# Claiming every SBUF slot in a fixed order before a two-layer hybrid decoder trunk starts

## The chip, the cores and the metric

The kernel runs on one core of a Trainium2 chip. The metric is the device time of one execution in microseconds (us). Engines are named as in the profile: PE is TensorE (matmuls), PEld its weight loads, DVE is VectorE, ACT is ScalarE, POOL is GpSimd, SP is SyncE, which here only issues DMAs.

## The reference

Two layers work on one sequence of 256 tokens, 1,024 channels wide, in float32. Each layer is a token mixer and a feed-forward block, both behind an RMSNorm:

```python
h = rmsnorm(x, norm_mix[l]); proj = h @ w_in[l]          # 1024 -> 5956 columns, split in 12 parts
y_attn = dsa_attention(aq, ak, av, iq, ik, iw)           # 8 heads of 64; an indexer picks 64 keys per query
o = hgrn2_chunked(silu(hq), k_in, hi, log_f)             # gated linear recurrence, 4 heads, state 128 x 128
y_hgrn = rmsnorm(o, hgrn_norm[l]) * silu(hg)
merged = sigmoid(ga) * (y_attn @ w_proj_attn[l]) + sigmoid(gb) * (y_hgrn @ w_proj_hgrn[l])
x = x + merged @ w_out[l]                                # 1024 -> 1024
h = rmsnorm(x, norm_ffn[l])
g, u = split(h @ w_ffn_in[l])                            # 1024 -> 2 x 2816
x = x + (silu(g) * u) @ w_ffn_out[l]                     # 2816 -> 1024
```

## The kernel before, in words

**Tiling.** The 256 tokens are two blocks `i` of 128. All products with the model's weights go through one pattern. `take()` brings a chunk of a weight matrix into SBUF by DMA (`w`, 128 partitions x 2,048 float32, 8 KB per partition), ACT rounds it to `hi` (float32r), and DVE writes the rest `lo = w - hi`. The activations are held transposed and split in the same way: `hT`, `h2T`, `yT`, `mT` and `act`, each a hi and a lo part. `mm3` then issues three matmuls per slice, hi x hi, hi x lo and lo x hi, to get nearly float32 precision out of the fast float32r mode.

**Who reads what.** In these matmuls the *activations are the stationary operand* (PEld loads a 128 x 128 slice of them, 512 bytes per partition, before every matmul, 188 ns by the profile) and the *weights `hi` and `lo` are the moving operand* (512 columns, 2,048 bytes per partition). A row of the trace such as `fi<-hi,h2T_lo` therefore reads: output `fi`, moving `hi`, stationary `h2T_lo`. For each layer there are 1,512 such matmuls of 512 columns, 3,024 in all, and 48 of 324 columns (`idx`, 96 in all).

**Stages of a layer, by the names of their outputs.** `idx`, `aq`, `ak`, `hf`, `hq`, `av`, `vh`, `hg`, `ga`, `gb` (parts of the input projection, with the attention and the recurrence in between); `pj` (the two output projections of the mixer, stationary `yT`); `wo` (stationary `mT`); `fi` (feed-forward in, 528 matmuls, stationary `h2T`); `fo` (feed-forward out, 264 matmuls, 24 for each of eleven tiles `act`).

**Order.** The program is first recorded. `Program.schedule` then simulates it, picks the order of the instructions, and gives every tile a *slot* of its tag: three slots each for `w`, `hi` and `lo`, eight (4 KB) for the stationary pairs (tag `hT`), fourteen (4 KB) for large tiles (tag `s4`, which holds `act` among others), six for 2 KB tiles (`s2`), fourteen for small vectors (`sm`). `emit` then walks through that order and asks the tile pool for each tile as it comes up, with the tag and the slot as its key. The pool places a key in SBUF when it first sees it, behind what it has placed before. So the addresses before follow from the order in which the schedule first touches each slot: constants of 8, 32 or 64 bytes stand between the large tiles.

Line 442 in the trace is the line of `emit` that issues every recorded call, so nearly all rows carry it; the tiles' names tell the rows apart.

Of the kernel before, what the change touches and what calls it, by code (L numbers as in the profile page):

```python
# [8 lines left out]
BF16 = mybir.dt.bfloat16  # L9
F32 = mybir.dt.float32  # L10
F32R = mybir.dt.float32r
I32 = mybir.dt.int32
U8 = mybir.dt.uint8
# [140 lines left out]
class Program:  # L154
# [54 lines left out]
    def price(self, op, eng, name, out, args, kw):  # L209
# [23 lines left out]
        n = max([n] + [v.size for v in ins])  # L233
        if name in ("tensor_copy", "tensor_scalar") and not any(v.t.tag in PSUM_TAGS for v in ins if isinstance(v, View)):
            return 65.0 + n * 0.52
# [190 lines left out]
        return self.span  # L426


    def emit(self, tc):
        nc = tc.nc  # L430
        engines = {"DVE": nc.vector, "ACT": nc.scalar, "PE": nc.tensor, "SP": nc.sync, "POOL": nc.gpsimd}
        with ExitStack() as ctx:
            sb = ctx.enter_context(tc.tile_pool(name="sb", bufs=1))
            ps = ctx.enter_context(tc.tile_pool(name="ps", bufs=1, space=PSUM))
            ctx.enter_context(tc.manual_schedule())
            real = lambda v: v.resolve() if isinstance(v, View) else v
            for o in self.order:
                for t in o.first:
                    pool = ps if t.tag in PSUM_TAGS else sb
                    t.handle = pool.tile([128] + list(t.shape), t.dtype, tag=f"{t.tag}_{t.slot}", name=t.name)  # L440
                for name, a, k in o.calls:
                    getattr(engines[o.eng], name)(*[real(x) for x in a], **{n: real(x) for n, x in k.items()})  # L442


PSUM_TAGS = ("P", "Q")
SLOTS = {"w": 3, "hi": 3, "lo": 3, "hT": 8, "s4": 14, "s2": 6, "sm": 14, "work": 2, "bias": 2, "rqs": 4,
         "gbc": 2, "P": 4, "Q": 4}
TUNING = {"stretch": 1.5, "bonus": 3000.0, "slack": 4000.0}
# [727 lines left out]
```

## Time and profile before

| | before |
|---|---|
| median of 3 runs | 821.86 us (820.89 to 822.17) |
| the profiled execution's own time | 822.42 us |
| its span, first to last instruction | 820.5 us |
| outside the span | 1.9 us |
| PE busy | 807.7 us (98%), 3,982 matmul records |
| PEld busy | 659.8 us (80%) |
| DVE busy | 537.8 us (66%) |
| ACT busy | 403.2 us (49%) |
| DMA | 139.66 MB, 51% of 16 engines' time |

Matmuls are pipelined: a matmul of 512 columns has a record of 387 to 401 ns, yet the next one starts 227 to 235 ns later. The pace of PE is therefore read from the *starts* of successive matmuls, not from their durations. In the timeline a row "x3" is three matmuls of the same kind that follow each other, and in the chain view a row "x36" is 36 matmuls back to back, with the time from the first start to the next work's start.

### The profile page before, as it was taken

How to read it: one execution, taken by the hardware profiler on the slowest of the kernel's cores; microseconds unless marked ns; L12 is line 12 of the kernel's file. 1: busy time of each engine (PE TensorE's matmuls, PEld its weight loads, DVE VectorE, ACT ScalarE, POOL GpSimd, SP SyncE). 2: the span in 40 equal slices, each digit the busy share in tenths (PEclk: the TensorE clock that was granted, in tenths of full speed). 3: DMA queues.
4: the chain of work that ended last, by engine and by line, in shares of the span. 5: the costliest groups of instructions: out<-in, count | busy, mean ns of one | idle time of the engine just before them, and what ended most of it. 6: DMA issues, size and time to landing. Idle time of an engine off the chain costs nothing.

```text
span 820.5 us, 10255 instructions
## 1 busy us (share of the span) xinstructions
PE 807.7 (98%) x3982; PEld 659.8 (80%) x3982; DVE 537.8 (66%) x947; ACT 403.2 (49%) x518; POOL 5.3 (1%) x13
## 2 busy tenths in 40 slices
PE   7999999999999999999999999999999999999998
PEld 5887788888878888888887778888887888888886
DVE  5999855677775454554488998566868645556442
ACT  5765855343364445452346676533435544445330
POOL 2000000000000000000000000000000000000000
PEclk7999999999999999999999999999999999999999
DMA  8645455333656556546546365543354665655531
GB/s 277 207 148 203 146 174 196 103 112 123 218 190 204 175 185 194 167 153 206 166 154 231 103 206 189 170 146 112 103 195 155 214 198 166 201 179 180 175 133 51
DMA packets 86224, 139.66 MB, mean 170 GB/s; under 512 B 3214, under 2 KB 50480, under 8 KB 86176
## 3 DMA queue, kind: packets, MB, share of 16 engines
q1 hardware_dynamic: 85856, 138.53, 50.9%
q0 software_dynamic: 320, 0.48, 0.3%
q8 instruction: 31, 0.51, 0.3%
q14 instruction: 17, 0.14, 0.0%
HBM read 137.95 MB, written 1.05 MB: 169 GB/s over the span
## 4 chain that ended last, share of the span: by engine, by line
PE 89%; DVE 6%; issue 2%; ACT 2%; DMA 1%; POOL 0%; DVEq 0%; POOLq 0%
PE fi L442 29%; PE fo L442 15%; PE pj L442 5%; PE gb L442 5%; PE wo L442 5%; PE ga L442 4%; PE av L442 3%; PE aq L442 3%; PE hg L442 3%; PE vh L442 3%; PE hq L442 2%; DVE lo L442 2%; PE ak L442 2%; PE idx L442 2%; PE hf L442 1%
## 5 line engine op out<-in xcount | busy, mean ns | idle before, releaser
L442 DVE TENSOR_TENSOR lo<-w,hi 128x2048 fp32r<-128x2048 f32 (+3 forms) x134 | 295.0, 2202 | 222.0 <-ACT hi L442 221.6
L442 ACT ACTIVATE hi<-w 128x2048 fp32r<-128x2048 f32 (+3 forms) x134 | 247.4, 1846 | 284.7 <-PE fi L442 96.4
L442 PE MATMUL fi<-hi,h2T_hi 128*128 128x512 f32 x352 | 141.1, 401 | 0.2
L442 PE MATMUL fi<-hi,h2T_lo 128*128 128x512 f32 x352 | 138.2, 393 | 0.0
L442 PE MATMUL fi<-lo,h2T_hi 128*128 128x512 f32 x352 | 137.7, 391 | 0.0
L442 PE MATMUL fo<-hi,act 128*128 128x512 f32 x352 | 111.4, 395 | 0.0
L442 PEld LDWEIGHTS fi<-hi,h2T_lo 128*128 128x128 f32 x352 | 66.1, 188 | 15.3 <-DVE h2T_lo L442 0.7
L442 PEld LDWEIGHTS fo<-hi,act 128*128 128x128 f32 x352 | 66.1, 188 | 14.9
L442 PEld LDWEIGHTS fi<-hi,h2T_hi 128*128 128x128 f32 x352 | 66.1, 188 | 13.8 <-DVE h2T_lo L442 0.8
L442 PEld LDWEIGHTS fi<-lo,h2T_hi 128*128 128x128 f32 x352 | 66.2, 188 | 13.2
L442 PE MATMUL fo<-lo,act 128*128 128x512 f32 x176 | 69.1, 392 | 0.0
L442 PEld LDWEIGHTS fo<-lo,act 128*128 128x128 f32 x176 | 33.1, 188 | 7.4
L442 PE MATMUL gb<-hi,hT_hi 128*128 128x512 f32 x64 | 26.8, 418 | 0.0
L442 PE MATMUL pj<-hi,yT_hi 128*128 128x512 f32 x64 | 26.0, 407 | 0.0
L442 PE MATMUL wo<-hi,mT_hi 128*128 128x512 f32 x64 | 25.8, 404 | 0.0
L442 PE MATMUL ga<-hi,hT_hi 128*128 128x512 f32 x64 | 25.7, 402 | 0.0
L442 PE MATMUL pj<-hi,yT_lo 128*128 128x512 f32 x64 | 25.3, 395 | 0.0
L442 PE MATMUL pj<-lo,yT_hi 128*128 128x512 f32 x64 | 25.2, 394 | 0.0
L442 PE MATMUL gb<-hi,hT_lo 128*128 128x512 f32 x64 | 25.2, 393 | 0.0
L442 PE MATMUL ga<-hi,hT_lo 128*128 128x512 f32 x64 | 25.1, 393 | 0.0
L442 PE MATMUL wo<-lo,mT_hi 128*128 128x512 f32 x64 | 25.1, 392 | 0.0
L442 PE MATMUL ga<-lo,hT_hi 128*128 128x512 f32 x64 | 25.1, 392 | 0.0
(346 smaller groups left out, 1309.9 us busy)
## 6 DMA issues: line engine op xcount, KB each, us to landing
w<-in_w_ffn_in_dram SPq DMA_DIRECT2D x88, 512.0 KB, 4.7
w<-in_w_in_dram SPq DMA_DIRECT2D x42, 1024.0 KB, 5.1
w<-in_w_ffn_out_dram SPq DMA_DIRECT2D x22, 1024.0 KB, 4.7
w<-in_w_out_dram SPq DMA_DIRECT2D x8, 1024.0 KB, 4.7
w<-in_w_proj_attn_dram SPq DMA_DIRECT2D x4, 1024.0 KB, 4.9
w<-in_w_proj_hgrn_dram SPq DMA_DIRECT2D x4, 1024.0 KB, 4.9
w<-in_w_in_dram SPq DMA_DIRECT2D x4, 512.0 KB, 11.4
w<-in_w_in_dram SPq DMA_DIRECT2D x4, 324.0 KB, 10.8
```

What stands on the lines that cost most here:

```text
L442: getattr(engines[o.eng], name)(*[real(x) for x in a], **{n: real(x) for n, x in k.items()})
```

## The change

A new method `homes` runs at the head of `emit`. It asks the pool once for every SBUF slot, in an order of its own, before any instruction is issued: first small slots up to address 24,576 (with a pad up to exactly that address), then the slots of `w`, `hi`, `lo`, `hT`, `s4` and `gbc`, then everything else from large to small. The tiles that `emit` asks for later find their key already placed. The schedule, the slots, the instructions of every engine, their order and their waits are the same as before, instruction by instruction; only addresses differ.

```diff
+    def homes(self, pool):
+        size = {}
+        for tag, q in self.queue.items():
+            for t in q:
+                if tag not in PSUM_TAGS:
+                    key = (tag, t.slot)
+                    size[key] = max(size.get(key, 0), t.n * SIZE.get(t.dtype, 4))
+        big = [k for tag in ("w", "hi", "lo", "hT", "s4", "gbc") for k in sorted(size) if k[0] == tag]
+        rest = sorted((k for k in size if k not in big), key=lambda k: (size[k], k))
+        at, low = BASE, []
+        for k in rest:
+            n = -(-size[k] // 32) * 32
+            if at + n <= ORIGIN:
+                low.append((k, size[k]))
+                at += n
+        low.reverse()
+        named = {k for k, _ in low}
+        if at < ORIGIN:
+            low.append((("pad", 0), ORIGIN - at))
+        for (tag, slot), n in low + [(k, size[k]) for k in big + [k for k in reversed(rest) if k not in named]]:
+            pool.tile([128, -(-n // 4)], F32, tag=f"{tag}_{slot}", name=f"home_{tag}{slot}")
...
             real = lambda v: v.resolve() if isinstance(v, View) else v
+            self.homes(sb)
             for o in self.order:
...
+SIZE = {U8: 1, BF16: 2}
+BASE, ORIGIN = 16512, 24576
```

The addresses of what PE reads in the 3,024 large matmuls, taken from the two built programs. A byte address counts within a partition; "remainder" is the address modulo 128. Slices of a stationary tile lie 512 bytes apart and columns of a moving tile 2,048 bytes, so the remainder of a slot is that of all its slices.

| operand | slots before (hex) | remainder before | slots after (hex) | remainder after |
|---|---|---|---|---|
| moving `hi` | 1abc0, 1e4c0, 244c0 | 64 | c000, e000, 10000 | 0 |
| moving `lo` | 204c0, 224c0, 264c0 | 64 | 12000, 14000, 16000 | 0 |
| stationary, tag `hT`, four slots | 107c0, 137c0, 19bc0, 1cbc0 | 64 | 18000 to 1f000 in steps of 1000 | 0 |
| stationary, tag `hT`, the other four | 2bbe0, 2cbe0, 31be0, 32be0 | 96 | (the same range) | 0 |
| stationary `act`, tag `s4` | d3c0, e3c0, f7c0, 147c0 | 64 | 20000 to 2b000 in steps of 1000 | 0 |
| stationary `act`, tag `s4` | a380, b380 | 0 | (the same range) | 0 |
| stationary `act`, tag `s4` | 8360, 9360, 2dbe0, 2ebe0, 2fbe0, 30be0 | 96 | (the same range) | 0 |

By the slots that the schedule gave, the stationary operand of the 3,024 matmuls has these remainders before: 64 in 1,944 of them, 0 in 72, and 96 in 1,008. The 1,008 are: in layer 0, the whole of `pj` (96), half of `wo` (48) and of `fi` (264), and 132 of `fo`; in layer 1, half of the ten input projections but `idx` (264: 24 each of `aq`, `ak`, `hf`, `hq`, `av`, `vh`, `hg` and 48 each of `ga` and `gb`), half of `pj` (48), and 156 of `fo`. In `fi` and `wo` of layer 1 there are none.

## Rows read from the trace of the kernel before

**Rows 1.** The page: engines' busy time, share of the span, instructions; the granted clock.

```profile
PE 807.7 (98%) x3982; PEld 659.8 (80%) x3982; DVE 537.8 (66%) x947; ACT 403.2 (49%) x518; POOL 5.3 (1%) x13
...
PEclk7999999999999999999999999999999999999999
```

**Rows 2.** The page: the chain that ended last, by engine.

```profile
PE 89%; DVE 6%; issue 2%; ACT 2%; DMA 1%; POOL 0%; DVEq 0%; POOLq 0%
```

**Rows 3.** Waits: who waited for whom, us in total, times, longest.

```profile
DVE lo L442 <- ACT hi L442: 221.6, 91, 5.7
ACT hi L442 <- PE fi L442: 96.4, 42, 3.9
```

**Rows 4.** The chain, layer 0, `fi`: start us, us, what.

```profile
232.57 3.06 PE fi L442 x12
...
236.06 39.42 PE fi L442 x171
...
278.70 8.29 PE fi L442 x36
...
356.31 1.45 PE fo L442 x6
```

**Rows 5.** The chain, layer 1, the same pieces of `fi`.

```profile
633.22 3.02 PE fi L442 x12
...
636.67 38.82 PE fi L442 x171
...
678.70 8.19 PE fi L442 x36
...
755.59 1.46 PE fo L442 x6
```

**Rows 6.** The chain, layer 0: a stretch of `ga` and one of `pj`.

```profile
116.71 8.16 PE ga L442 x36
...
194.22 9.81 PE pj L442 x42
```

**Rows 7.** PE's timeline in `fo`: start us, us; stationary remainder 96, tile `act3`.

```profile
374.05 0.86 PE L442 MATMUL fo<-hi,act 128*128 128x512 f32 x3
...
376.85 0.86 PE L442 MATMUL fo<-hi,act 128*128 128x512 f32 x3
```

**Rows 8.** The same, remainder 0, tile `act4`.

```profile
379.64 0.85 PE L442 MATMUL fo<-hi,act 128*128 128x512 f32 x3
...
382.39 0.85 PE L442 MATMUL fo<-hi,act 128*128 128x512 f32 x3
```

**Rows 9.** The same, remainder 64, tile `act6`.

```profile
392.11 0.84 PE L442 MATMUL fo<-hi,act 128*128 128x512 f32 x3
...
394.83 0.84 PE L442 MATMUL fo<-hi,act 128*128 128x512 f32 x3
```

**Rows 10.** PE's timeline behind transposes, `fi` of layer 1, remainder 64.

```profile
636.74 0.40 PE L442 MATMUL fi<-lo,h2T_hi 128*128 128x512 f32 x1
...
638.60 0.39 PE L442 MATMUL fi<-hi,h2T_hi 128*128 128x512 f32 x1
...
640.87 0.39 PE L442 MATMUL fi<-lo,h2T_hi 128*128 128x512 f32 x1
```

**Rows 11.** Windows at both clock levels: us, PE busy (x instructions), PEclk, DMA share, GB/s.

```profile
64.10:67.30 3.20, 3.20 (x9) 0.50 0.73 229
...
636.00:676.00 40.00, 40.00 (x181) 1.00 0.63 202
```

**Rows 12.** PE's timeline at the lower clock: `hq`, 512 columns.

```profile
64.22 0.63 PE L442 MATMUL hq<-lo,hT_hi 128*128 128x512 f32 x1
...
66.78 0.63 PE L442 MATMUL hq<-lo,hT_hi 128*128 128x512 f32 x1
```

**Rows 13.** PE's timeline: `idx`, 324 columns, layer 1, full clock, remainder 96.

```profile
419.06 0.31 PE L442 MATMUL idx<-hi,hT_lo 128*128 128x324 f32 x1
...
422.03 0.31 PE L442 MATMUL idx<-lo,hT_hi 128*128 128x324 f32 x1
```

**Rows 14.** All loads and conversions of one kind: ns min/median/max, first and last start us.

```profile
L442 PEld LDWEIGHTS fo<-lo,act x176: 187/188/192, 356.2 to 815.9; 128*128 128x128 f32 x176
...
L442 DVE TENSOR_TENSOR lo<-w,hi x134: 822/2293/2295, 13.9 to 802.0; 128x2048 fp32r<-128x2048 f32 x124, 128x648 fp32r<-128x648 f32 x4, 128x1024 fp32r<-128x1024 f32 x4, 128x1296 fp32r<-128x1296 f32 x2
```

**Rows 15.** Windows of `fi`, layer 0: us, busy PE, PEld, DVE, ACT, POOL, PEclk, DMA share.

```profile
232.50:356.00 123.50, 123.43 (x558) 100.49 (x559) 68.61 (x78) 56.67 (x64) 0.00 (x0) 1.00 0.59 189
```

## The prediction

> **What bounds the kernel now.** I read the page first. PE is busy for 98% of the span and the clock is full in all but the first slices [rows 1]; the chain that ended last runs over PE for 89% [rows 2]. Then the waits: DVE waits for ACT, and ACT for PE to give a buffer back [rows 3]. In `fi` of layer 0 PE has 123.43 of 123.50 us, DVE 68.61 and ACT 56.67, DMA a share of 0.59 [rows 15]. So PE sets the pace, and almost any nanosecond that a matmul saves shortens the run. What is left is the pace itself, read from the distance of starts.
>
> **That pace depends on where the stationary operand lies.** Three tiles of `fo` are used one after the other by the same code. The two rows of each group enclose 12 matmuls:
> - remainder 96: 376.85 - 374.05 = 2.80 us, 233.3 ns each [rows 7];
> - remainder 0: 382.39 - 379.64 = 2.75 us, 229.2 ns [rows 8];
> - remainder 64: 394.83 - 392.11 = 2.72 us, 226.7 ns [rows 9].
>
> Other stages agree: `pj` of layer 0 (remainder 96 throughout) takes 9.81 / 42 = 233.6 ns, `ga` of layer 0 (64 throughout) 8.16 / 36 = 226.7 ns [rows 6]. `fi` is the cleanest pair, because both layers run the same pieces: 171 matmuls take 39.42 us in layer 0, where 84 of them have remainder 96, and 38.82 us in layer 1, where none has [rows 4, 5].
>
> All moving operands have remainder 64 before. So remainder 64 is not the roundest address, it is the one that *agrees with the moving operand*; the rounder 0 is slower by 2.5 ns. I read this as: two streams out of SBUF get in each other's way least when both sit at the same place within a block of 128 bytes. The weight load itself lasts 187 to 192 ns wherever its tile lies [rows 14], so it is the matmul stream that gives way.
>
> By the Trainium skill, "SBUF — State Buffer", section "Who interferes with whom", PE has two independent read ports and never waits on anyone, so an address could not change its pace. The trace disagrees, by 6.6 ns between rows 7 and 9; the measurement decides, and the page's rule stays as a rival below.
>
> **The change part by part.**
>
> 1. *Instructions, waits, queues: nothing moves.* Every engine has the same instructions in the same order with the same waits, and the extra pool requests issue nothing. Cost 0.
>
> 2. *1,008 matmuls go from remainder 96 against 64 to 0 against 0.* After the change, stationary and moving agree everywhere, the condition of the fast row. Three prices:
>  - steady rows: 233.3 - 226.7 = 6.6 ns, times 1,008 = 6.7 us. This is too much, since a matmul with agreeing operands is not always at its fast pace: just behind transposes, 8 of them took 638.60 - 636.74 = 1.86 us, 232.5 ns each, and only the next 10 took 2.27 us, 227.0 ns [rows 10].
>  - one piece of `fi`: (39.42 - 38.82) / 84 = 7.1 ns, giving 7.2 us; the short piece (8.29 - 8.19) / 18 = 5.6 ns, giving 5.6 us [rows 4, 5].
>  - the whole of `fi`, from its first matmul to the first of `fo`: 356.31 - 232.57 = 123.74 us in layer 0, 755.59 - 633.22 = 122.37 us in layer 1 [rows 4, 5]. The 1.37 us belong to 264 matmuls, 5.2 ns each, giving 5.2 us.
>
>  I take the last, since it has the interruptions in it as they fall.
>
> 3. *72 matmuls go from 0 against 64 to 0 against 0*: 229.2 - 226.7 = 2.5 ns, 0.2 us.
>
> 4. *1,944 matmuls go from 64 against 64 to 0 against 0.* No row shows both at 0. Lower bound: worse by 6.6 ns each, as the slowest row. Upper bound: all that keeps them above the array's own pace. At the half-speed level (1.2 GHz) [rows 11] six matmuls take 66.78 - 64.22 = 2.56 us, 426.7 ns [rows 12]; half of that is 213.3 ns at 2.4 GHz, against 226.7. So 13.3 ns could go. I take 0: the extra is as large for `idx`, where 20 matmuls of 324 columns take 422.03 - 419.06 = 2.97 us, 148.5 ns [rows 13], against 213.3 x 324 / 512 = 135.0 ns, that is 13.5 ns. Its moving rows are 1,296 bytes apart, so they start 0, 16, 32 or 48 bytes past a multiple of 64. An extra that ignores both the length and that start looks like a fixed price of changing weights.
>
> 5. *`idx`* (96 matmuls): [rows 13] is a stretch with remainder 96 and already shows the general price; 0.
>
> 6. *ACT, DVE, DMA.* The full-size conversions last between the median 2,293 and the maximum 2,295 ns for the most part, in three different slots of each tag [rows 14]. Where a slot moves they change by 0, and DVE's idle time in `fi` (123.50 - 68.61 us) covers far more [rows 15]. DMA transfers are covered in the same way at a share of 0.59. When PE is 1% faster these engines become due 1% sooner, and none is near its limit there.
>
> Sum: 5.2 + 0.2 = 5.4 us. The profiled execution's 822.4 us become 817.0; it lies 0.6 us above the median of 821.86, so I state 816.5 us as the median. This case alone spans 814.5 to 818: 7.2 + 0.2 us by the highest price of point 2, and 4 us if a quarter of the gain is lost where PE waits for the attention or the recurrence.
>
> **The rivals.**
>
> - *Half of the extra goes too (13%).* The moving tiles now start on multiples of 2,048 and the weight slices on multiples of 512, where none stood before; each slice then no longer straddles two blocks of 512 bytes. If that halves the 13.3 ns: 3,024 x 6.7 = 20.2 us more, 816.5 - 20.2 = 796.3 us. For it: nothing before lies at a multiple of 512. Against: rows 13.
> - *All of it goes (8%).* 3,024 x 13.3 = 40.2 us more, 776.3 us. For it: at half clock the extra is absent [rows 12], so it is not the array's own. By the Trainium skill, "TensorE: Matmul & The Clock Gate", section "Back-to-back issue gap", a warm matmul of 512 columns needs N / 2.4 + 2.5, an estimate of 215.8 ns; by that page the time would be about 783 us. No row here reaches it: 226.7 is the best steady pace.
> - *It is the place and not the agreement (7%).* Remainder 96 is found mostly at high addresses (2bbe0 upwards) and at 8360 and 9360; the fast slots lie in between. If the region decided, `hT` at 18000 to 1ffff would gain its 720 x 5.2 = 3.7 us, while `act` at 20000 and above would all be slow: 168 of the 528 in `fo` lose 5.2 ns, 0.9 us, and 72 lose 4.1, 0.3 us. Net 2.5 us, 819.4 us. For it: `act4` (b380) and `act6` (f7c0) differ in both, place and remainder [rows 8, 9]. Against: 8360 and 9360 lie far from 2dbe0, and a region would have to be slow at both ends.
> - *No effect (7%).* The rows' difference comes from something else that goes with the tiles, as the engines that work beside them, and addresses don't matter: 821.9 us. That is what the page on SBUF would have, by the rule above. Against: rows 7 and 9 run the same code on the same engines within 21 us.
> - *Slower (5%).* Both streams now begin at the very start of a 512-byte and a 128-byte block at once. If that is where they collide most, all matmuls run at the slow row's 233.3 ns: 1,944 x 5.2 + 72 x 4.1 = 10.4 us, 832.3 us. It decides once more than about 1,040 of the 3,024 (5.4 us / 5.2 ns) turn slow. Against: before, the two also begin at the same place within 128 bytes, and that is the fast case.
>
> **How the numbers follow.** The forecast has 60%. A measurement of this kernel can tell about 0.2% (1.6 us) from no change. Faster: 60 + 13 + 8 + 7 = 88%; same: 7%; slower: 5%. The range leaves out the full gain, no effect and slower, 20% together: 795 us, just under the half gain, to 820.5 us, just over the place rival. The forecast alone spans 814.5 to 818.
>
> **What would show each step.** In `fi` the 171 and 36 matmuls should take the same in both layers, near 38.8 and 8.2 us; twelve matmuls of `fo` 2.72 us for every `act`; `pj` of layer 0 about 9.6 us for 42. PE's instructions, the full-size DVE conversion (2,293 ns) and the load (188 ns) should not change. If the pace falls below 226 ns, the extra was an address's doing and the first two rivals are right. If some `fo` tiles stay at 233 ns, the place rival is.

## The result, and the profile after

| | before | changed |
|---|---|---|
| median of 4 runs | 821.38 us (820.71 to 822.17) | 817.06 us (815.58 to 817.61) |
| the profiled execution's own time | 822.42 us | 817.03 us |
| its span | 820.5 us | 815.2 us |
| PE busy | 807.7 us | 802.3 us |

The ratio is 0.9944 with a 95% interval of 0.9927 to 0.9961: the kernel became faster, by 3.2 to 6.0 us of 821.38. A second measurement of the same kernel in five rounds gave 0.9942 (0.9929 to 0.9954). The forecast was 816.5 us, with 5.4 us gained; the two profiled executions are 5.4 us apart, the medians 4.3. Both profiled executions have one short stretch at the half clock after 60 us (before: [rows 11]; changed: the windows view in the next section), so their difference doesn't come from it.

The page of the changed kernel, engines' busy time:

```profile
PE 802.3 (98%) x3982; PEld 659.5 (81%) x3982; DVE 537.5 (66%) x947; ACT 403.0 (49%) x518; POOL 5.3 (1%) x13
```

Against [rows 1] the instruction counts are equal and PE alone became shorter, by 5.4 us. DVE and ACT moved by 0.3 us or less. So the time came out of the matmuls. The chain of the changed kernel, the same pieces as in [rows 4] and [rows 6] (layer 0):

```profile
116.20 8.16 PE ga L467 x36
...
193.50 9.57 PE pj L467 x42
...
231.54 3.02 PE fi L467 x12
...
235.00 38.77 PE fi L467 x171
...
276.99 8.20 PE fi L467 x36
...
353.92 1.21 PE fo L467 x5
```

and as in [rows 5] (layer 1):

```profile
513.49 8.16 PE ga L467 x36
...
590.83 9.58 PE pj L467 x42
...
628.86 3.03 PE fi L467 x12
...
632.33 38.77 PE fi L467 x171
...
674.32 8.20 PE fi L467 x36
...
751.25 1.44 PE fo L467 x6
```

Before, `fi` took 39.42 us for its 171 matmuls in layer 0 and 38.82 in layer 1. Now it takes 38.77 in both. The whole of `fi`, from its first matmul to the first of `fo`, takes 353.92 - 231.54 = 122.38 us in layer 0 and 751.25 - 628.86 = 122.39 in layer 1. So layer 0 lost its 1.4 us, and layer 1, where all operands had agreed before, gained nothing. `pj` of layer 0 went from 9.81 to 9.57 us. `ga` of layer 0, which had agreed before, stayed at 8.16. The layers have become alike, as they compute the same.

PE's timeline in `fo` of layer 0: two starts with twelve matmuls between them, as in [rows 7 to 9].

```profile
368.59 0.84 PE L467 MATMUL fo<-hi,act 128*128 128x512 f32 x3
...
371.31 0.84 PE L467 MATMUL fo<-hi,act 128*128 128x512 f32 x3
```

371.31 - 368.59 = 2.72 us: 226.7 ns each, the pace of the best tile before, in a stretch whose tiles stood at 233.3 ns before. The next rows of that timeline repeat the step of 1.36 us for six. All loads and conversions of one kind, as in [rows 14]:

```profile
L467 PEld LDWEIGHTS fo<-lo,act x176: 187/188/192, 353.8 to 810.6; 128*128 128x128 f32 x176
...
L467 DVE TENSOR_TENSOR lo<-w,hi x134: 816/2292/2295, 13.5 to 797.1; 128x2048 fp32r<-128x2048 f32 x124, 128x648 fp32r<-128x648 f32 x4, 128x1024 fp32r<-128x1024 f32 x4, 128x1296 fp32r<-128x1296 f32 x2
```

At their new addresses the load's median is 188 ns as before, and the conversion's 2,292 ns against 2,293.

### The profile page after: what moved, and what is told of

Its sections match the earlier page's. It is cut to its first block, busy times and chain, and to the rows that moved or that the text cites. A ratio compares the mean times of both kernels' runs of the same rounds, so it can differ in the third digit from the quotient of the medians.

```text
span 815.2 us, 10255 instructions
## 1 busy us (share of the span) xinstructions
PE 802.3 (98%) x3982; PEld 659.5 (81%) x3982; DVE 537.5 (66%) x947; ACT 403.0 (49%) x518; POOL 5.3 (1%) x13
## 4 chain that ended last, share of the span: by engine, by line
PE 89%; DVE 6%; issue 2%; ACT 2%; DMA 1%; POOL 0%; DVEq 0%; POOLq 0%
PE fi L467 29%; PE fo L467 15%; PE pj L467 5%; PE gb L467 5%; PE wo L467 5%; PE ga L467 4%; PE av L467 3%; PE aq L467 3%; PE hg L467 3%; PE vh L467 3%; PE hq L467 2%; DVE lo L467 2%; PE ak L467 2%; PE idx L467 2%; PE hf L467 1%
## 5 line engine op out<-in xcount | busy, mean ns | idle before, releaser
L467 PE MATMUL gb<-lo,hT_hi 128*128 128x512 f32 x64 | 25.0, 391 | 0.0
```

## The experiments

Three theories stood against each other. **A**: the stationary operand has to *agree* with the moving one. **B**: an operand has to stand at a round address by itself. **C**: the region of SBUF decides. The first four kernels move slots of the changed kernel, by a gap ahead of the first slot of a tag. The slots follow each other in the order `w`, `hi`, `lo`, `hT`, `s4`, so a gap moves its own tag and all that come behind it:

```diff
+        rows, seen = [], set()
+        for k in big + [k for k in reversed(rest) if k not in named]:
+            if k[0] in GAPS and k[0] not in seen:
+                rows.append((("gap", len(rows)), GAPS[k[0]]))
+            seen.add(k[0])
+            rows.append((k, size[k]))
-        for (tag, slot), n in low + [(k, size[k]) for k in big + [k for k in reversed(rest) if k not in named]]:
+        for (tag, slot), n in low + rows:
```

"Distance" below is the stationary address minus the moving one, modulo 256; "ahead" means that the stationary tile stands that many bytes above the moving one, "behind" that it stands below it. In the kernel before the distance was 0 in 1,944 of the large matmuls, 192 in the 72 with remainder 0, and in the 1,008 with remainder 96 it was 32 (912 of them) or 160 (96, all in `fo`). By the built program, the 288 of the 1,008 that are in `fo` are 144 in each layer.

A caution on spans first. A short stretch at the half clock, just behind a wait of PE for `hfraw` of 2.14 us, comes in some executions and not in others with the same wait. The windows view of 55 to 70 us, of the changed kernel:

```profile
55.00:70.00 15.00, 12.86 (x57) 0.89 0.43 140
```

and of the first experiment, where it is absent:

```profile
55.00:70.00 15.00, 12.06 (x59) 1.00 0.40 137
```

There the span is 1.4 us shorter (813.8 against 815.2) at the same paces. The stretch is also absent from the kernels below at 64, 128 and 16 bytes ahead and at 16 behind, and present in all others. So the experiments are read by their pace in `fi` (171 matmuls, changed kernel 38.77 us) and in `fo` of layer 1 (258 matmuls, changed kernel 58.56 us, 227.0 ns each), and by the span only where a difference is larger.

**All operands at 32, agreeing.**

```diff
+GAPS = {'w': 32}
```

> The changed kernel with 32 bytes put ahead of the slots of w, so that moving and stationary operands of all 3,024 large matmuls lie at remainder 32 (modulo 128) and agree. Theory A (what counts is that the stationary operand agrees with the moving one within a block of 128 bytes): as the changed kernel, span 815 us, steady pace 226.7 ns. Theory B (the address itself counts: a stationary slice must begin on a multiple of 64 bytes): all matmuls at the slow pace of 233.3 ns, 5.2 ns x 3,024 = 15.7 us more, span 831 us. Theory C (the region of SBUF counts): 815 us.

Measured 815.65 us, span 813.8. The chain:

```profile
234.04 38.82 PE fi L473 x171
...
751.48 58.55 PE fo L473 x258
```

B falls: no operand stands on a multiple of 64, and the pace is that of the changed kernel.

**Stationary operands 32 bytes ahead.**

```diff
+GAPS = {'hT': 32}
```

> The changed kernel with 32 bytes put ahead of the slots of hT: all moving operands at remainder 0, all stationary ones at 32. Theories A and B: every large matmul slow, steady pace 233.3 ns, span 815.2 + 15.7 = 831 us. Theory C (region) and no effect of addresses: 815 us.

Measured 831.07 us, span 829.2, 14.0 us above the changed kernel where 15.7 was expected. The chain:

```profile
238.68 39.89 PE fi L473 x171
...
765.23 60.21 PE fo L473 x258
```

60.21 / 258 = 233.4 ns, the slow pace of [rows 7], now in every stage. C and "no effect" fall: no tile moved by more than 32 bytes. Beside the kernel before it, this one also refutes that the stationary operand's own address alone counts: in both the stationary tiles stand at the same addresses, and only the moving ones differ.

**Stationary operands 64 bytes ahead.**

```diff
+GAPS = {'hT': 64}
```

> The changed kernel with 64 bytes put ahead of the slots of hT: moving at remainder 0, stationary at 64. Theory A: the pace of the kernel before where the two differed by 64, 229.2 ns steady, that is 2.5 ns x 3,024 = 7.6 us more, less some 2 us in matmuls that are not at the steady pace: span 821 to 823 us. Theory B: a stationary slice at 64 is as good as at 0, 815 us.

Measured 830.62 us, span 828.8. The chain:

```profile
237.73 39.90 PE fi L473 x171
...
764.82 60.22 PE fo L473 x258
```

A in its form of 128 bytes misses: the full price, 233.4 ns, where 229.2 was expected. The tiles that cost 229.2 before [rows 8] stood 64 bytes *behind* the moving operand, not ahead. Modulo 128 the two are the same; so the rule is not one of 128 bytes.

**Moving operands 32 bytes ahead.**

```diff
+GAPS = {'hi': 32, 'hT': 96}
```

> The changed kernel with the moving operands alone at remainder 32 (32 bytes ahead of hi, 96 behind lo), the stationary ones at 0. Theory A: the two differ by 32 the other way round, steady pace 233.3 ns, span 831 us. Theory B (only the stationary operand's own address counts): 815 us.

Measured 834.0 us, span 832.2; the stationary operands stand at 128 modulo 256 here, with the moving ones at 32, distance 96. The chain:

```profile
239.41 40.05 PE fi L473 x171
...
767.98 60.46 PE fo L473 x258
```

The slowest of all, 234.3 ns, where B, with the stationary operands on multiples of 64, expected the best pace. Since they moved too, from 0 to 128 modulo 256, the first two runs are the cleaner test of B.

With A in need of a new form, the next runs ask for its period, its slope, and the region.

**128 bytes ahead.**

```diff
+GAPS = {'hT': 128}
```

> The changed kernel with 128 bytes put ahead of the slots of hT: all stationary operands 128 bytes past the moving ones (modulo 256). Theory A0 (agreement modulo 128, as the prediction put it): the fast pace of 226.7 ns, span 815 us. Theory A1 (agreement modulo 256: before, 64 bytes behind cost 229.2 ns, with 64 bytes ahead all 3,024 cost 233.3 ns, which one rule modulo 128 can't give): some slower pace, 229 to 234 ns, span 822 to 832 us. If the pace falls below 226 ns, agreement is not the best place and a better layout exists.

Measured 827.97 us, span 826.1. The chain:

```profile
236.50 39.73 PE fi L473 x171
...
762.30 59.98 PE fo L473 x258
```

232.5 ns: agreement modulo 128 is worth 0.9 ns of the 6.4 that agreement is worth in `fo`.

**192 bytes ahead, which is 64 behind modulo 256.**

```diff
+GAPS = {'hT': 192}
```

> The changed kernel with 192 bytes put ahead of the slots of hT, so that stationary operands stand at 192 against 0, 64 bytes behind the moving ones modulo 256, as the tiles act4 and act10 did before. Theory A0 (modulo 128): as with 64 bytes ahead, 233.3 ns, span 829 us. Theory A1 (modulo 256): 229.0 ns as in the kernel before, 2.3 ns x 3,024 = 7 us more than the changed kernel at most, span 820 to 822 us.

Measured 820.66 us, span 818.8. The chain:

```profile
236.18 39.15 PE fi L473 x171
...
756.01 59.07 PE fo L473 x258
```

59.07 / 258 = 229.0 ns, the pace of [rows 8] for all 3,024. The moving tiles stood at 192 in the kernel before and stand at 0 here; the distance is the same, and so is the pace. With the run at 64 ahead this rules out a period of 128 bytes: 64 behind is cheap and 64 ahead is not. Nor is it 512: in the kernel before, every `lo` slot lay 256 bytes modulo 512 from the stationary tiles that `ga` of layer 0 read, in the changed kernel 0, and `ga` took 8.16 us for 36 in both. A period of 256 bytes fits every run.

**16 bytes ahead, for the tiles of tag hT.** Each slot of hT gets 256 bytes more, and the tile begins 16 bytes into it:

```diff
+                    if t.tag == "hT":
+                        room = pool.tile([128, t.n + 64], t.dtype, tag=f"{t.tag}_{t.slot}", name=t.name)
+                        t.handle = room[:, SHIFT // 4:SHIFT // 4 + t.n].rearrange("p (k t) -> p k t", t=128)
...
+SHIFT = 16
```

> The changed kernel with the tiles of tag hT (2,496 of the large matmuls) moved by 16 bytes against the moving operands, act left where it agrees. If the loss grows with the distance: a pace of some 230 ns in all stages but fo, span 823 us. If any disagreement costs the full price: 233.3 ns there, 226.7 ns in fo, 2,496 x 5.2 = 13 us more, span 828 us. If blocks of 64 bytes are all that counts: 226.7 ns, 815 us.

Measured 824.81 us, span 823.0. The chain:

```profile
189.89 4.09 PE pj L477 x18
...
209.73 15.36 PE wo L477 x66
...
236.41 39.90 PE fi L477 x171
...
591.31 4.20 PE pj L477 x18
...
611.25 14.98 PE wo L477 x66
...
760.72 58.52 PE fo L477 x258
```

Sixteen bytes cost the full price in `fi` (233.3 ns), while `fo`, whose operands agree, keeps 226.8. But not everywhere: 18 matmuls of `pj` took 4.09 us in layer 0 (227.2 ns each) and 4.20 in layer 1 (233.3 ns), at the same distance. In `wo` it is the other way round: 66 matmuls took 15.36 us in layer 0 and 14.98 in layer 1. So at 16 bytes there are two paces, and a stretch runs mostly at one or the other; what decides which was not found. The span of 823.0 us that the first expectation names comes about in another way: not by one pace of 230 ns, but by a mix of the two.

**16 bytes behind, for the tiles of tag hT.**

```diff
+SHIFT = 240
```

> The changed kernel with the tiles of tag hT (2,496 of the large matmuls) at 240 modulo 256 against moving operands at 0, that is 16 bytes behind; act agrees. If the sign counts (64 behind cost 229.0 ns, 64 ahead 233.3, 16 ahead mostly 233): 227 to 229 ns in all stages but fo, span 815 to 821 us. If the size alone counts: 233 ns there, span 823 to 829 us. fo at 226.9 ns by both.

Measured 815.95 us, span 814.2. The chain:

```profile
233.98 38.78 PE fi L477 x171
...
631.11 39.06 PE fi L477 x171
```

226.8 ns in layer 0, 228.4 in layer 1: almost nothing lost. Against the kernel at 32 agreeing, which also lacks the stretch at the half clock, the span is 0.4 us longer; at 16 bytes ahead it was 9.2 us longer. The sign counts.

**The large slots in the reverse order.**

```diff
-        big = [k for tag in ("w", "hi", "lo", "hT", "s4", "gbc") for k in sorted(size) if k[0] == tag]
+        big = [k for tag in ("gbc", "s4", "hT", "lo", "hi", "w") for k in sorted(size) if k[0] == tag]
```

> The changed kernel with the order of the large slots turned round: act lowest (8000 to 13000 hex), hT at 14000 to 1b000, lo, hi and w above; all still at multiples of 4,096. Theories A (agreement) and B (the address's remainder): as the changed kernel, 226.7 ns in every stage, span 815 us. Theory C (the region counts): with act at 8000 to 13000, where the tiles 8360 and 9360 were slow before, fo would show paces up to 233 ns, up to 3 us more.

Measured 817.81 us, span 815.9. The chain:

```profile
235.73 38.77 PE fi L473 x171
...
753.58 58.56 PE fo L473 x258
```

The same 38.77 and 58.56 us, with `act` at the bottom of the range. C falls.

**The price of one stage alone.** Only act disagrees, by 32 bytes.

```diff
+GAPS = {'s4': 32}
```

> The changed kernel with 32 bytes put ahead of the slots of s4 alone: act disagrees by 32 bytes, hT agrees. If every matmul pays for itself and nothing else covers it: fo's 528 matmuls at 233.2 ns instead of 226.9, 6.3 ns x 528 = 3.3 us more, span 818 to 819 us, all other stages as in the changed kernel (fi 227.9 ns). If a part of the price is hidden in the whole: less than 2 us.

Measured 820.61 us, span 818.7, 3.5 us above the changed kernel's; both executions have the stretch at the half clock. The chain:

```profile
234.82 38.82 PE fi L473 x171
...
754.77 60.20 PE fo L473 x258
```

`fo` pays (60.20 - 58.56) / 258 = 6.4 ns a matmul, times 528 = 3.4 us, and the span grows by that. No part of it is hidden.

**Pads alone.** The kernel before, with its slots in the order of before, and a pad ahead of those that don't stand at 192 modulo 256:

```diff
+        at, seen, pads = BASE, set(), 0
+        for o in self.order:
+            for t in o.first:
+                key = (t.tag, t.slot)
+                if t.tag in PSUM_TAGS or key in seen:
+                    continue
+                seen.add(key)
+                if t.tag in ("hi", "lo", "hT", "s4") and (192 - at) % 256:
+                    pool.tile([128, (192 - at) % 256 // 4], F32, tag=f"pad_{pads}", name=f"pad{pads}")
+                    at, pads = at + (192 - at) % 256, pads + 1
+                pool.tile([128, -(-size[key] // 4)], F32, tag=f"{t.tag}_{t.slot}", name=f"home_{t.tag}{t.slot}")
+                at += -(-size[key] // 32) * 32
```

> The kernel before, its slots in the order of before, with nothing but pads ahead of those slots of hi, lo, hT and s4 that need one, so that all of them lie at 192 modulo 256. Agreement alone, without multiples of 512, 2,048 or 4,096 and without the new order. Theory A1: the whole gain, 226.7 ns steady, ratio to before 0.9945 (0.993 to 0.996), as the changed kernel. If the multiples or the order gave a part: between 0.995 and 1.

Measured 817.08 us, ratio 0.9949 (0.9936 to 0.9963). The chain:

```profile
234.45 38.82 PE fi L465 x171
...
752.42 58.54 PE fo L465 x258
```

Beside it on the same chip, the changed kernel:

> The changed kernel as it is, beside the padded one on the same chip. Theory A1: the same ratio as the padded kernel within 0.15%, both near 0.9945. If multiples or order matter as well: this one is faster by more than that.

Measured 816.78 us, ratio 0.9942 (0.9929 to 0.9954). The ratios lie within 0.07% of each other, and the padded kernel's pieces of `fi` and `fo` differ by 0.05 us or less from the changed kernel's 38.77 and 58.56. The gain is that of agreement; multiples of 512, 2,048 or 4,096 and the new order give nothing that these runs can tell.

One distance more stands in the kernel before. Its tile `act5` of layer 0 lay at 8360 against moving tiles at 192 modulo 256, distance 160. PE's timeline, two starts with twelve matmuls between them:

```profile
385.16 0.86 PE L442 MATMUL fo<-hi,act 128*128 128x512 f32 x3
...
387.96 0.86 PE L442 MATMUL fo<-hi,act 128*128 128x512 f32 x3
```

Paces by distance, from `fo` of layer 1 where act was moved and from `fi` of layer 0 where hT alone was:

| distance | kernel | pace, ns |
|---|---|---|
| 0 | changed | 58.56 / 258 = 227.0 |
| 16 | 16 ahead | 39.90 / 171 = 233.3 |
| 32 | 32 ahead | 60.21 / 258 = 233.4 |
| 64 | 64 ahead | 60.22 / 258 = 233.4 |
| 96 | moving at 32, stationary at 128 | 60.46 / 258 = 234.3 |
| 128 | 128 ahead | 59.98 / 258 = 232.5 |
| 160 | before, `act5` of layer 0 | 2.80 / 12 = 233.3 |
| 192 | 64 behind | 59.07 / 258 = 229.0 |
| 240 | 16 behind | 38.78 / 171 = 226.8 |

## Why the prediction was right

*What bounds the kernel.* Right. PE got 5.4 us shorter and the profiled execution with it; in the run where act alone disagreed, 3.4 us of dearer matmuls made 3.5 us of span. One reading was too wide: the clock was not full in all but the first slices, since [rows 11] have it at half from 64.1 to 67.3 us; nothing in the sum hung on it.

*Point 1, nothing else moves.* Right: equal instruction counts, and ACT and DVE within 0.3 us.

*Points 2 and 3, the gain of 5.2 + 0.2 us.* Right in size, and the choice among the three prices was the right one. The whole of `fi` in layer 0 fell from 123.74 to 122.38 us, by the 1.4 us that the price was taken from. The steady rows' 6.7 us and the 7.2 us of one piece of `fi` would have been too much for a profiled gain of 5.4 us. Carrying one price of 5.2 ns to all stages was rougher than it looks: `fo` paid 6.4 ns a matmul where act alone disagreed, while 32 bytes of distance in all 3,024 cost 14.0 us, 4.6 ns each, by which the 1,008 would give 4.7 us. By the medians the gain is 4.3 us, by the ratios 3.2 to 6.0, so 5.4 lies in the upper half.

*Point 4, 0 against 0 is no better than 64 against 64.* Right: no run had a steady pace below 226.7 ns (8.16 / 36 in `ga`, before and after). The rivals of half or all of the extra going fell with it. The reason given for it, that the 13.3 ns are a fixed price of changing weights, was not tried and stays open.

*Points 5 and 6, `idx`, ACT, DVE and DMA.* Right: `idx` kept its pace even at 32 bytes (last section), the conversion's median is 2,292 ns against 2,293, and no engine but PE changed by more than 0.3 us.

*"The same place within a block of 128 bytes".* This is the step that was wrong, and by luck it cost nothing: the change happens to make the operands agree modulo 256 as well. Had it put them 128 bytes apart, the same rule would have forecast the best pace, and 232.5 ns would have come. It was read from one price for 64 bytes behind, taken as a price for 64 bytes apart. The runs showed 233.4 ns for 64 ahead, 232.5 for 128 and 229.0 for 64 behind.

*The rivals.* The place rival fell with the reversed order, and no effect with the 14 us that 32 bytes cost. Slower fell with the result: both at 0 is a fast case.

What stays open is why: no run tells what the two streams share that has a period of 256 bytes and a direction.

## What to carry to other kernels

Where PE bounds a kernel, read the pace from the starts of matmuls by tile. Where two tiles run the same code at different paces, compare their addresses. Here, float32r matmuls of 512 columns ran best when the stationary tile stood at the moving tile's address modulo 256 or 16 bytes behind it; a few small constants between large tiles had cost 4 to 5 us of 821, and pads alone gave that back.

## What the runs showed of the hardware that had not been expected

The price goes by the distance modulo 256 and has a direction: 16 bytes behind is free to within 1.7 ns, 16 bytes ahead mostly costs 6.5. At 16 bytes ahead the same code runs at two paces, 227.2 and 233.3 ns, in two stretches of one execution.

The matmuls of 324 columns didn't pay. In the kernel with stationary operands 32 bytes ahead, PE's timeline of `idx` in layer 1 has these rows:

```profile
423.29 0.31 PE L473 MATMUL idx<-hi,hT_lo 128*128 128x324 f32 x1
...
424.77 0.31 PE L473 MATMUL idx<-hi,hT_hi 128*128 128x324 f32 x1
...
425.21 0.31 PE L473 MATMUL idx<-hi,hT_hi 128*128 128x324 f32 x1
...
425.65 0.31 PE L473 MATMUL idx<-hi,hT_hi 128*128 128x324 f32 x1
...
426.11 0.31 PE L473 MATMUL idx<-hi,hT_hi 128*128 128x324 f32 x1
426.25 0.31 PE L473 MATMUL idx<-lo,hT_hi 128*128 128x324 f32 x1
```

From the first row to the last, 20 matmuls in 2.96 us, 148.0 ns, against 148.5 in [rows 13], whose tile stood 32 bytes ahead as well. In the changed kernel, where the first slices agree, 20 of them take as long, 418.43 - 415.46 = 2.97 us:

```profile
415.46 0.32 PE L467 MATMUL idx<-lo,hT_hi 128*128 128x324 f32 x1
...
418.43 0.31 PE L467 MATMUL idx<-hi,hT_hi 128*128 128x324 f32 x1
```

The moving rows stand 1,296 bytes apart, so the distance changes from slice to slice, at 32 bytes ahead 32, 16, 0 and 240 in turn. Yet three matmuls at 32 took 425.21 - 424.77 = 0.44 us, three at 16 took 0.44 and three at 0 took 0.46, so a single slice at 32 pays nothing. Whether that is because the distance doesn't stay, or because the matmuls are shorter, was not tried.
